# Preparing the state-space parameters of a two-block transformer: phase tables grouped ahead of the matrices, their stores on GpSimd's queue, and another buffer for the transposed weights

## The chip, the core and the metric

One core of a Trainium2 chip runs the whole program in one launch. The time is device microseconds of that core, the median of several executions. One further execution is recorded by the hardware profiler; all rows shown are from that one. Engines: PE is TensorE's matmul, PEld its weight load, DVE is VectorE, ACT is ScalarE, POOL is GpSimd, SP is SyncE, which here only issues DMAs.

## The reference

Two blocks of two layers each work on a sequence of 512 tokens, 2048 wide. The first block has an attention layer (gated linear attention beside "forgetting" attention) and then a diagonal state-space layer, S5; the second block has a recurrent layer and a latent-attention layer. The change concerns only the parameters of S5: 128 groups of 16 channels, each with a complex diagonal state of 64.

```python
def s5_ssm(u, lam_re, lam_im, log_step, b_re, b_im, c_re, c_im, d):
    lr = jnp.minimum(lam_re, -1e-4); li = lam_im
    step = jnp.exp(log_step)[:, None]
    mag = jnp.exp(lr * step)
    lb_re, lb_im = mag * jnp.cos(li * step), mag * jnp.sin(li * step)
    den = lr * lr + li * li
    nr, ni = lb_re - 1.0, lb_im
    coef_re = (nr * lr + ni * li) / den
    coef_im = (ni * lr - nr * li) / den
    bb_re = coef_re[..., None] * b_re - coef_im[..., None] * b_im
    bb_im = coef_re[..., None] * b_im + coef_im[..., None] * b_re
    ...  # x_t = lb * x_{t-1} + bb u_t (complex), y_t = Re(c x_t) + d u_t
```

All of lb, coef, bb and the powers of lb depend on weights alone, so the kernel can prepare them while an earlier layer still runs.

## The kernel before

**Staging.** Almost all time goes to projections, 2048-wide matrix products in split fp32r: a weight piece `wraw` (256 KB) is loaded by SP (line 265), ACT writes its rounded part and DVE the remainder into `whl` (`wpiece`, `split`: ACT first, then DVE), and PE makes three products from hi and lo parts into PSUM tiles `pj`. `wraw` has 3 buffers, `whl` 4, `pj` 4. `chunkF` uses two `pj` tiles at a time; `chunkT` uses all four. When a chunk is done, DVE or ACT evacuates it (`ha<-pj,bc` for queries and keys, `ge<-pj,bc` for gates).

**Order.** The program is traced in the order of the Python calls; a planner then fixes the order on each engine and DMA queue ahead of time, with its own durations: it takes, whenever an engine is free in its plan, the earliest traced instruction that is ready. Each engine and each queue works strictly in that order. A DMA issue is an instruction of its engine: it waits, at its place, for the data that it stores or for the buffer that it fills, and all behind it waits too. Tiles of one tag share that tag's buffers; the next user waits until the last reader of the old tile is done, DMAs included.

**The work around the change.** In the attention layer `layer_ab` calls a hook `beside(o)`, which is `params(o)` in `emit`, at fixed places: o = 0 before the first output gates; o = 1 to 8 in a loop over four pairs of forgetting-attention heads (`fox(i)`, then o = 1+2i; then two gate chunks for i = 1, 2 and `fox_in(i+1)`, the projections of the next pair, for i < 3; then o = 2+2i); o = 9 to 12 after each of the last four gate chunks; and o = 13 to 20 after each of the eight chunks of the output projection `w_out`. `params` makes three kinds of work:

- `s5_params` (o = 0), on GpSimd mostly: angles, powers, coefficients; a transposed weights table (`W` through PE into `wrow`, tag `ha` with 8 buffers, stored by 16 small DMAs from ACT's queue at line 930); and 16 rows of a table `s5tab` in DRAM, staged in `wt` and stored by GpSimd (line 983).
- `s5_tables(b0)`, eight calls: loads two rows of `s5tab` into the one buffer `lm` (SP, line 995), and for each of two batches DVE makes a table of cosines `C` and one of sines `Sn` (four products of 512 columns from `lm` into `cst` and `acc`, one subtraction and one addition into `hc`, 4 buffers). ACT's queue stores both (lines 1011 and 1012) as `s5ph`.
- `s5_batch_params(b)`, sixteen batches, in two halves. First half: loads (SP, lines 1023 to 1032), matrices on GpSimd through `cst` and `hc`, stored by GpSimd itself (line 1051), on DVE through `acc2`, and `BB` in the tag `fac` (one buffer). Second half: 32 small matmuls on PE that read `fac` (listed as tr<-vs,fac and tr<-acc,fac), and stores. It is traced at the next call, bound behind the last `chunkF` matmul that was traced before (`net.last`). A batch holds two of the four `vs` buffers.

`lm` also holds the masks of the gated linear attention; their last use is before the forgetting attention begins.

Of the kernel before, what the change touches and what calls it, by code (L numbers as in the profile page):

```python
# [22 lines left out]
P = 128  # L23
# [76 lines left out]
class Net:  # L100
# [723 lines left out]
    def s5_params(self):  # L824


        nc, I, A = self.nc, self.I, ALU
# [90 lines left out]
        for half in range(2):  # L918
            pw_ = self.ps("tr")
            for i in range(2):  # L920
                for j in range(2):
                    s_ = 2 * half + j
                    o = (2 * i + j) * P
                    self.tr(pw_[0:64, o:o + P], N[8 + i] if s_ == 3 else W[:, i, s_])
            wrow = self.t("ha", [64, 2, 2, P])
            self.act(wrow.rearrange("p i j f -> p (i j f)"), pw_[0:64])
            for j in range(2):
                for gg in range(2):
                    for i in range(2):
                        nc.scalar.dma_start(self.wtab[:, gg, 2 * half + j, i],  # L930
                                           wrow[:, i, j, 64 * gg:64 * gg + 64])
# [58 lines left out]
    def s5_tables(self, b0):  # L990


        nc, A = self.nc, ALU
        tab = self.t("lm", [P, S])[:, 0:384].rearrange("p (b f) -> p b f", b=2)
        self.dma.dma_start(tab, self.s5tab[b0:b0 + 2, :, 0:192].rearrange("b p f -> p b f"))
        for b in range(2):
            Tb = tab[:, b, 0:128].rearrange("p (i n q) -> p i n q", i=2, q=4)
            Ta = tab[:, b, 128:192].rearrange("p (i n q) -> p i n q", i=2, q=4)
            C, Sn = self.hd("hc"), self.hd("hc")
            u = [self.t("cst", [P, S]), self.t("acc", [P, S])]  # L1000
            v4 = lambda ap: ap.rearrange("p (q a b) -> p q a b", q=4, a=8)
            av = lambda i: Ta[:, i].rearrange("p n q -> p q n").unsqueeze(3).to_broadcast([P, 4, 8, 16])
            bv = lambda i: Tb[:, i].rearrange("p n q -> p q n").unsqueeze(2).to_broadcast([P, 4, 8, 16])
            self.tt(v4(u[0]), av(0), bv(0), A.mult)
            self.tt(v4(u[1]), av(1), bv(1), A.mult)
            self.tt(C, u[0], u[1], A.subtract)
            self.tt(v4(u[0]), av(0), bv(1), A.mult)
            self.tt(v4(u[1]), av(1), bv(0), A.mult)
            self.tt(Sn, u[0], u[1], A.add)
            d = self.dp.tile([P, 2, S], F32, name=self.name("s5ph"))  # L1010
            nc.scalar.dma_start(d[:, 0], C)
            nc.scalar.dma_start(d[:, 1], Sn)
            self.s5ph.append(d)

    def s5_batch_params(self, b):
# [533 lines left out]
def emit(nc, tc, I, col, out, layers=("ab", "c", "even", "odd")):  # L1549
    with ExitStack() as ctx:  # L1550
        net = Net(nc, tc, ctx, I, col)
        raws = net.load_x(I["x"])
        tok = bc = fac = acc2 = None
        second = "even" in layers or "odd" in layers
        last = layers[-1]
        end = lambda name: dict(store=False) if name == last else {}


        pending = []

        def params(o):


            if o == 0:
                net.s5_params()
            elif o <= 8:
                net.s5_tables(2 * (o - 1))
            for b in pending:
                with net.after([net.last]):
                    next(b, None)  # L1570
            pending.clear()
            if 3 <= o < 19:
                pending.append(net.s5_batch_params(o - 3))
                next(pending[0])
        if "ab" in layers:
            h = net.layer_ab(raws, beside=params if "c" in layers else None)
            raws, acc, _ = net.w_out(h, I["ab_w_out"][0], beside=params if "c" in layers else None, **end("ab"))
        else:
            acc = net.sumsq(raws)
        if "c" in layers:  # L1580
            if "ab" not in layers:
                net.s5_params()
                for b in range(16):
                    if b % 2 == 0:
                        net.s5_tables(b)
                    for _ in net.s5_batch_params(b):
                        pass
            h = net.layer_c(raws, acc)
            raws, acc, acc2 = net.w_out(h, I["c_w_out"][0], perm=True, fold="fin_g" if second else None, **end("c"))
        if second:  # L1590
            if acc2 is not None:
                t1 = net.rsqrt(net.colsum(acc), D)
                fac = net.bcast(t1, net.t("fac", [P, S]))
                sq = net.t("tk", [P, 4])
                net.tt(sq, t1, t1, ALU.mult)
                tok = net.rsqrt(net.colsum(acc2), D, mul=sq)
                net.tt(tok, tok, t1, ALU.mult)
                bc = net.bcast(tok)
            else:
                tok, bc = net.norm(acc)  # L1600
            if "even" in layers:
                h = net.layer_even(raws, tok, bc)
                raws, acc, _ = net.w_out(h, I["l0_w_out_2"], fac=fac, **end("even"))
                fac = None
                tok, bc = net.norm(acc) if "odd" in layers else (None, None)
            if "odd" in layers:
                h = net.layer_odd(raws, tok, bc)
                raws, acc, _ = net.w_out(h, I["l1_w_out_2"], fac=fac, **end("odd"))
        net.final_out(raws, acc, "fin2" if second else "fin_g", out)
# [12 lines left out]
```

## Time and profile before

| | |
|---|---|
| median of 3 runs | 3428.4 us (3428.11 to 3428.41) |
| profiled execution: its time | 3427.85 us |
| profiled execution: span of its instructions | 3426.1 us |
| mean granted TensorE clock | 0.995 |
| busy share PE, PEld, DVE, ACT, POOL | 98%, 82%, 56%, 39%, 23% |
| instructions | 49372 |

A busy PE is not always a PE at its peak, since the ends of matmuls are modelled; so what a stage loses is read from the stretches in which PE is not busy, from the named waits of PE, and from the granted clock. The S5 parameters are prepared between about 328 and 965 us of the span.

### The profile page before, as it was taken

The page shows a single profiled execution, that of the slowest core. Times are in us where ns is not written, and L with a number is a line of the kernel's source. Part 1 is how long each engine was busy: PE and PEld are TensorE (multiplying, and loading weights), DVE is VectorE, ACT ScalarE, POOL GpSimd, SP SyncE. Part 2 cuts the span into 40 slices and gives each one's busy share as a digit, 9 for nine tenths or more (in the row PEclk, how much of TensorE's full clock was granted, in tenths as well). Part 3 has the DMA queues.
Part 4 walks back from the last instruction along what each step waited for, and adds up shares of the span by engine and source line. Part 5 has one row for each costly group of instructions (what it writes and reads, how often), then busy time and mean ns, then how long its engine had stood idle before and what let it go on. Part 6 is the DMA issues. An engine that isn't in the chain of part 4 may idle for free.

```text
span 3426.1 us, 49372 instructions
## 1 busy us (share of the span) xinstructions
PE 3359.1 (98%) x18156; PEld 2812.7 (82%) x18156; DVE 1905.6 (56%) x3213; ACT 1336.7 (39%) x2497; POOL 786.3 (23%) x974
## 2 busy tenths in 40 slices
PE   8999989999999999999999999999999999999997
PEld 7898678877899989888888777888888888888885
DVE  5763674588567665734345655453545545646534
ACT  4443232233343333423343554232434444445422
POOL 0341851158614222100122010012110121112011
PEclk9999999999999999999999999999999999999998
DMA  5223354576734444333443223334333223232333
GB/s 149 75 63 88 99 157 121 146 211 194 220 118 145 133 135 127 114 120 118 135 135 96 69 70 86 96 119 143 108 87 83 66 75 80 79 82 78 110 118 108
DMA packets 407203, 390.23 MB, mean 114 GB/s; under 512 B 66713, under 2 KB 364057, under 8 KB 406961
## 3 DMA queue, kind: packets, MB, share of 16 engines
q1 hardware_dynamic: 381168, 354.64, 36.2%
q10 hardware_dynamic: 22464, 22.12, 1.9%
q0 software_dynamic: 3328, 10.32, 0.8%
q8 instruction: 142, 2.33, 0.3%
q14 instruction: 101, 0.82, 0.1%
HBM read 340.71 MB, written 46.25 MB: 113 GB/s over the span
## 4 chain that ended last, share of the span: by engine, by line
PE 83%; DVE 6%; POOL 4%; DMA 3%; issue 2%; ACT 1%; SPq 0%; DVEq 0%; ACTq 0%; POOLq 0%
PE pj L152 74%; PE sc L152 4%; PE po L152 3%; PE tr L156 1%; DVE whl L140 1%; DVE wk L140 1%; POOL vs L140 1%; DVE acc L140 1%; POOL hc L140 1%; DMA gated<-ge 1%; DMA wraw<-in_ab_w_in_dram 1%; POOL fac L140 1%; POOL cst L140 0%; PE tr L152 0%; POOL acc L140 0%
## 5 line engine op out<-in xcount | busy, mean ns | idle before, releaser
L152 PE MATMUL pj<-hl,whl 128*128 128x512 f32 x10224 | 2453.2, 398 | 12.3 <-ACT whl L137 6.9
L152 PEld LDWEIGHTS pj<-hl,whl 128*128 128x128 f32 x10224 | 1911.8, 189 | 453.7 <-DVE whl L140 7.7
L140 DVE TENSOR_TENSOR whl<-wraw,whl 128x512 fp32r<-128x512 f32 (+2 forms) x1064 | 806.9, 762 | 1096.3 <-ACT whl L137 1090.4
L137 ACT ACTIVATE whl<-wraw 128x512 fp32r<-128x512 f32 (+2 forms) x1064 | 660.0, 623 | 1332.9 <-PE pj L152 1072.3
L152 PE MATMUL pj<-whl,hl 128*128 128x256 f32 (+1 forms) x3840 | 482.1, 286 | 11.3 <-DVE ha L140 7.0
L152 PEld LDWEIGHTS pj<-whl,hl 128*128 128x128 f32 x3840 | 470.2, 190 | 17.8 <-DVE ha L140 7.2
L140 POOL TENSOR_TENSOR acc<-acc,wt 128x512 f32<-128x512 f32 x73 | 103.2, 1421 | 851.5 <-ACT wt L137 850.3
L140 POOL TENSOR_TENSOR ha<-wk,ha 64x512 fp32r<-64x512 f32 x32 | 44.6, 1394 | 294.6 <-ACT ha L137 256.2
L140 POOL TENSOR_TENSOR wt<-wt,acc 64x508 f32<-64x508 f32 x32 | 60.4, 1888 | 186.1 <-DVE wt L140 115.7
L137 ACT ACTIVATE wk<-sc,sm 128x256 f32<-128x256 f32 (+3 forms) x160 | 79.5, 501 | 60.1 <-DVE sm L148 55.1
L140 POOL TENSOR_TENSOR wt<-ha,wk 128x256 f32<-128x256 f32 x72 | 63.2, 905 | 113.4 <-PE pj L152 60.2
L152 PE MATMUL po<-pt,vs 128*128 128x128 f32 x560 | 80.2, 276 | 0.6 <-ACT pt L137 0.6
L156 PE MATMUL tr<-ident,wk 128*128 128x128 f32 x416 | 72.3, 276 | 7.7 <-ACT pt L137 6.5
L152 PEld LDWEIGHTS po<-pt,vs 128*128 128x128 f32 x560 | 72.9, 192 | 3.4 <-ACT pt L137 1.0
L152 PE MATMUL sc<-ha,ha 128*128 128x128 f32 (+1 forms) x224 | 72.0, 392 | 2.5 <-DVE sm L525 2.3
L137 ACT ACTIVATE pt<-tr 128x384 f32<-128x384 f32 (+3 forms) x96 | 46.6, 485 | 70.6 <-PE tr L156 54.2
L521 DVE TENSOR_REDUCE sm<-sc 128x1 f32<-128x128 f32 (+3 forms) x96 | 45.9, 488 | 47.5 <-PE sc L152 46.7
L156 PEld LDWEIGHTS tr<-ident,wk 128*128 128x128 f32 x416 | 51.7, 141 | 24.9 <-ACT pt L137 8.9
L140 POOL TENSOR_TENSOR fac<-vs,smb 128x128 f32<-128x128 f32 x64 | 37.9, 610 | 146.5 <-PE tr L152 139.4
L137 ACT ACTIVATE ge<-ge 128x512 f32<-128x512 f32 x64 | 40.1, 627 | 71.6 <-DVE ge L140 54.1
L143 DVE SCALAR_TENSOR_TENSOR ge<-ge,ge 128x512 f32<-128x512 f32 x60 | 45.9, 765 | 38.5 <-ACT ge L137 38.1
L140 POOL TENSOR_TENSOR fac<-wt,acc 128x512 fp32r<-128x512 f32 x8 | 10.3, 1292 | 236.0 <-ACT acc L137 179.2
(316 smaller groups left out, 3036.0 us busy)
## 6 DMA issues: line engine op xcount, KB each, us to landing
wraw<-in_l_w_in_dram SPq DMA_DIRECT2D x272, 256.0 KB, 2.8
wraw<-in_ab_w_in_dram SPq DMA_DIRECT2D x216, 256.0 KB, 2.9
wraw<-in_c_w_in_dram SPq DMA_DIRECT2D x128, 256.0 KB, 3.0
wraw<-in_l_w_out_dram SPq DMA_DIRECT2D x128, 256.0 KB, 2.7
wraw<-in_ab_w_out_dram SPq DMA_DIRECT2D x64, 256.0 KB, 3.8
wraw<-in_glu_w_dram SPq DMA_DIRECT2D x64, 256.0 KB, 2.7
wraw<-in_c_w_out_dram SPq DMA_DIRECT2D x64, 256.0 KB, 2.7
wraw<-in_l_w_in_dram SPq DMA_DIRECT2D x128, 128.0 KB, 2.3
```

Source lines behind the costliest of these rows:

```text
L137: return self.nc.scalar.activation(out, in_, func, **kw)
L140: return (eng or self.nc.vector).tensor_tensor(out, a, b, op=op)
L143: return self.nc.vector.scalar_tensor_tensor(out, a, s, b, op0=op0, op1=op1, **kw)
L152: return self.nc.tensor.matmul(out, l, r, start=start, stop=stop)
L156: return self.nc.tensor.transpose(out, in_, self.ident[:k, :k])
L521: self.nc.vector.tensor_reduce(mx, pb[:, 0:w], axis=AX.X, op=ALU.max)
```

## The change

Three edits. The transposed weights table `wrow` takes the tag `lm` (one buffer) in place of `ha` (eight). The stores of C and Sn are issued by GpSimd in place of ACT. And the hook's calendar changes: two calls of `s5_tables` at each of o = 1 to 4 in place of one at each of o = 1 to 8; then the batches, one at each of o = 5 to 18 and two at o = 10 and 12, in place of one at each of o = 3 to 18. The second halves still follow at the next call (the last at o = 19).

```diff
--- before.py
+++ after.py
@@ -922,7 +922,7 @@
                     s_ = 2 * half + j
                     o = (2 * i + j) * P
                     self.tr(pw_[0:64, o:o + P], N[8 + i] if s_ == 3 else W[:, i, s_])
-            wrow = self.t("ha", [64, 2, 2, P])
+            wrow = self.t("lm", [64, 2, 2, P])
             self.act(wrow.rearrange("p i j f -> p (i j f)"), pw_[0:64])
             for j in range(2):
                 for gg in range(2):
@@ -1008,8 +1008,8 @@
             self.tt(v4(u[1]), av(1), bv(0), A.mult)
             self.tt(Sn, u[0], u[1], A.add)
             d = self.dp.tile([P, 2, S], F32, name=self.name("s5ph"))
-            nc.scalar.dma_start(d[:, 0], C)
-            nc.scalar.dma_start(d[:, 1], Sn)
+            nc.gpsimd.dma_start(d[:, 0], C)
+            nc.gpsimd.dma_start(d[:, 1], Sn)
             self.s5ph.append(d)
 
     def s5_batch_params(self, b):
@@ -1557,21 +1557,25 @@
 
 
         pending = []
+        todo = iter(range(16))
 
         def params(o):
 
 
             if o == 0:
                 net.s5_params()
-            elif o <= 8:
-                net.s5_tables(2 * (o - 1))
-            for b in pending:
-                with net.after([net.last]):
-                    next(b, None)
-            pending.clear()
-            if 3 <= o < 19:
-                pending.append(net.s5_batch_params(o - 3))
-                next(pending[0])
+            elif o <= 4:
+                for i in range(2):
+                    net.s5_tables(4 * (o - 1) + 2 * i)
+            else:
+                for p in pending:
+                    with net.after([net.last]):
+                        next(p, None)
+                pending.clear()
+                for _, b in zip(range(2 if o in (10, 12) else 1), todo):
+                    p = net.s5_batch_params(b)
+                    next(p)
+                    pending.append(p)
         if "ab" in layers:
             h = net.layer_ab(raws, beside=params if "c" in layers else None)
             raws, acc, _ = net.w_out(h, I["ab_w_out"][0], beside=params if "c" in layers else None, **end("ab"))
```

## Rows read from the trace of the kernel before

**Rows 1.** Busy time of each engine by stretch, whole core

```profile
core 0: us, PE busy (x) PEld busy (x) DVE busy (x) ACT busy (x) POOL busy (x), PEclk, DMA share, GB/s
414.00:470.00 56.00, 43.50 (x261) 38.06 (x260) 46.54 (x58) 10.96 (x20) 42.47 (x82) 0.94 0.55 161
470.00:575.00 105.00, 105.00 (x593) 89.85 (x592) 51.90 (x102) 32.71 (x67) 12.56 (x22) 1.00 0.42 119
575.00:740.00 165.00, 162.07 (x980) 134.45 (x979) 114.15 (x216) 53.52 (x119) 47.10 (x76) 1.00 0.60 172
740.00:850.00 110.00, 102.06 (x625) 78.48 (x625) 87.32 (x117) 34.23 (x71) 89.79 (x133) 0.98 0.66 200
850.00:980.00 130.00, 130.00 (x708) 104.41 (x707) 77.67 (x110) 51.28 (x85) 68.77 (x92) 1.00 0.61 193
```

**Rows 2.** Who waited for whom, 400 to 470 us (total, times, longest)

```profile
ACT whl L137 <- DVE hc L140: 25.3, 7, 6.7
...
DVE cst L140 <- DMA lm<-s5tab: 10.9, 3, 7.0
...
PE pj L152 <- DVE ha L140: 7.0, 1, 7.0
...
PE tr L156 <- ACT pt L137: 3.5, 2, 1.8
...
PE pj L152 <- DVE whl L140: 1.3, 1, 1.3
...
PE po L152 <- ACT pt L137: 0.6, 1, 0.6
```

**Rows 3.** Timeline, 442.8 to 453.5 us (start, duration)

```profile
442.87 0.37 SPq L995 DMA_DIRECT2D lm<-s5tab  x1
...
446.75 1.13 DVE L140 TENSOR_TENSOR cst<-lm 128x512 f32<-128x512 f32 x1 [2.59 <-DMA lm<-s5tab]
...
452.22 0.68 DVE L140 TENSOR_TENSOR ha<-pj,bc 128x512 f32<-128x512 f32 x1
...
452.96 0.79 PE L152 MATMUL pj<-whl,hl 128*128 128x256 f32 x2 [7.05 <-DVE ha L140]
```

**Rows 4.** Granted clock in two short stretches

```profile
451.00:458.00 7.00, 5.04 (x24) 5.04 (x25) 6.93 (x10) 0.29 (x2) 5.33 (x9) 0.51 0.54 180
802.50:806.00 3.50, 3.50 (x10) 2.70 (x10) 3.50 (x6) 0.00 (x0) 3.38 (x6) 0.51 0.47 157
```

**Rows 5.** Who waited for whom, 580 to 740 us

```profile
POOL hc L1043 <- DMA s5ph<-hc: 32.3, 7, 7.0
...
PE tr L156 <- ACT pt L137: 2.9, 3, 1.4
```

**Rows 6.** Who waited for whom, 740 to 850 us

```profile
PE tr L152 <- POOL fac L140: 6.1, 5, 2.3
```

**Rows 7.** Instructions on tile fac by stretch (32 matmuls of PE for each batch)

```profile
737.00:824.00 87.00, 4.68 (x224) 3.15 (x224) 0.00 (x0) 0.00 (x0) 22.19 (x36) 0.98 0.65 192
824.00:966.00 142.00, 3.03 (x192) 2.22 (x192) 0.00 (x0) 0.00 (x0) 22.34 (x36) 1.00 0.67 210
```

**Rows 8.** Instructions on tile hc (ns minimum, median, maximum)

```profile
L140 DVE TENSOR_TENSOR hc<-cst,acc x32: 674/688/724, 417.3 to 731.1; 128x512 f32<-128x512 f32 x32
```

**Rows 9.** Tile s5d: the GpSimd stores

```profile
L1051 POOL DMA_DIRECT2D s5d<-hc x32: 580/580/675, 483.1 to 934.6; - x32
```

**Rows 10.** Instructions on tile lm by stretch

```profile
414.00:470.00 56.00, 0.00 (x0) 0.00 (x0) 26.52 (x25) 0.00 (x0) 0.94 0.55 161
...
575.00:740.00 165.00, 0.00 (x0) 0.00 (x0) 32.66 (x31) 0.00 (x0) 1.00 0.60 172
```

**Rows 11.** DMA issues, 330 to 980 us: KB each, median us to landing

```profile
s5ph<-hc ACTq DMA_DIRECT2D x32, 256.0 KB, 3.0
s5d<-hc POOLq DMA_DIRECT2D x32, 256.0 KB, 3.3
```

**Rows 12.** Tile s5w: the small stores of wrow, from issue to landing

```profile
DMA to landing us min/median/max: 1.7/1.8/2.1
```

## Prediction

> **What bounds the kernel now.** I read the granted clock and the busy shares first: PE is busy 98% of the span, so a change off PE can give back only what PE waits for. Then busy time by stretch [rows 1] shows where. From 414 to 470 us PE works 43.50 of 56 us, from 575 to 740 us 162.07 of 165, from 740 to 850 us 102.06 of 110; at 470 to 575 and 850 to 980 us it works throughout. So the S5 preparation costs PE 12.5 + 2.9 + 7.9 = 23.3 us of waiting, in the first, third and fourth stretch. To that comes the clock: after the long waits it stood at 0.51, the lower of its two levels (1.2 of 2.4 GHz), in 451 to 458 and 802.5 to 806 us [rows 4], where PE worked 5.04 and 3.50 us; at full clock these would have taken about half, so 2.5 and 1.7 us more are lost. Some 27 us, 0.8%, is all that the change could touch.
>
> Then the named waits. In 400 to 470 us [rows 2] PE waits 3.5 + 0.6 us for ACT's `pt`, 7.0 us for DVE's evacuation `ha` and 1.3 us for DVE's `whl`. ACT itself waits 25.3 us, seven times, for DVE's `hc`: these are the stores of C and Sn, which stand in ACT's queue ahead of the weight pieces and the `pt` copies and hold them until DVE has computed the table. DVE waits 10.9 us for the load of `lm`. The timeline [rows 3] shows both meeting: SP can issue the `lm` load at 442.87, when the old table has been read; DVE stands 2.59 us for it, then does two more table products before it reaches the evacuation at 452.22, and PE has stood 7.05 us. In 580 to 740 us [rows 5] ACT costs PE another 2.9 us, and GpSimd stands 32.3 us for `hc` buffers that table stores still read. In 740 to 850 us [rows 6] PE waits 6.1 us, five times, for GpSimd's `fac`: from 737 to 824 us seven batches pass (224 matmuls at 32), one per 12.4 us, against six in 142 us afterwards, one per 23.7 us [rows 7].
>
> **The change part by part.**
>
> *Stores on GpSimd.* 32 issues leave ACT. What PE loses by ACT's standing, 3.5 + 0.6 + 2.9 = 7.0 us [rows 2, 5], goes. Bounds: nothing, if the `pt` copies turn out to be late by DVE's own work anyway, and 7.0 + 1.3 us, if the late `whl` was also due to ACT. I take -7.0, since all of these waits stand in stretches with tables and [rows 2] names one cause for ACT. GpSimd gets 32 issues at 0.58 us by its own store of the same shape [rows 9], 18.6 us, and now waits for DVE in ACT's stead. What hides that: between 470 and 575 us it is busy 12.56 of 105 us [rows 1], and PE waits for it only where a batch's second half comes. Cover gone, it is a rival below. Behind a waiting store on GpSimd stand the staging copies for `s5tab`, and for these SP's `lm` loads.
>
> The store lands 3.3 us after a GpSimd issue and 3.0 us after an ACT issue [rows 11]; with four `hc` buffers and some 3 us of DVE work for each, that difference is worth nothing here. The Trainium skill (DMA: Bandwidth & Descriptors, SWDGE vs HWDGE vs iDMA) speaks against this edit: GpSimd writes its descriptors by software into SBUF, can be locked out there by DVE, and starts about 0.4 us later than a store by ACT. By the rows the sum has nothing for it; by the page an estimate is 32 times 0.4, or 13 us, if no store were hidden, and the sum below would end at 3431.
>
> *All tables first.* The order in which calls are traced is not the order of execution: the planner had already put 25 of the 64 table products into 414 to 470 us, and left 31 for after 575 [rows 10]. So half of the tables stay where they were. What moves into 470 to 575 us is 32.66 us of products and 16 of the 32 sums and differences at 0.688 us [rows 8], together 43.7 us of DVE, which has 51.90 of 105 us there [rows 1]: it fits, at 91%. The price of such density is read from 414 to 470 us, where DVE is 83% busy. Nearest is the late `whl`, 1.3 us in 56, so 2.4 us in 105; lower bound nothing, as PE waits for nothing in that stretch now; upper bound another stall like that of [rows 3] with its half clock, 7.0 + 2.5 = 9.5 us, since at the end of `fox_in(2)` a key chunk again hands over to a value chunk that wants all four `pj` tiles. I take +2.4.
>
> The stall at 445 us itself: its cause is DVE's order and the single `lm` buffer, and both stay. I take 0; the bound is -9.5 us, as the planner now orders DVE afresh and one evacuation placed two products earlier is enough.
>
> *Batches later.* Two effects. Tables no longer share `hc` and `cst` with batches after 575 us: GpSimd's 32.3 us of standing goes. And the calendar changes. Before, the fourth and fifth batch came only after the last tables, at 737 us or later, and with the next five made seven in 87 us. Now batches 0 to 2 have their second halves traced behind the key chunk of `fox_in(3)`, the others behind the gate chunks 9 (batch 3), 10 (4), 11 (5 and 6) and 12 (7), and the first two chunks of `w_out` (8 and 9, then 10). So the same 87 us should hold five batches or six. GpSimd's need is at most 12.5 us for each: 68.77 busy us of 130 [rows 1], by 23.7 us. Seven in 87 us are just that, five leave 17.4 us for each. The seven cost 6.1 + 1.7 = 7.8 us of waits and half clock, 1.1 us for each. I leave that price on two batches, 6 and 9, the second of each pair: `BB` has one buffer, so their products start only when the batch before has passed PE. That is 2.2 us, a gain of 5.6. Bounds: -7.8 (none waits, as with one per 23.7 us) and +7.8 (twice the waits, if the pairs and the late start bunch them).
>
> *`wrow` in `lm`.* The second half's copy must wait until the first half's eight stores have landed, 1.8 us after their issue [rows 12], at the head of ACT's queue. `whl` pieces stand ahead, so 0; bounds 0 and +1.8. The first table load into `lm` comes long after. That two `ha` buffers come free is worth nothing: no wait for a free `ha` buffer is among PE's.
>
> **Sum**, from the profiled execution's own time, 3427.85 us (its span is 3426.1; 1.75 us lie around it): -7.0 + 2.4 + 0 - 5.6 + 0 = -10.2, so 3417.65; the median of the runs is 0.55 us above the profiled one, so 3418.2, and I say 3418, 0.3% faster. About 0.2%, 6.9 us, is what a measurement of this kernel can tell from no change.
>
> **Rivals.**
>
> *The stall at 445 us goes too.* For it: [rows 3], any later place of two products lifts it. Against: the `lm` load is as late as before. 3418.2 - 9.5 = 3408.7 us.
>
> *DVE becomes the bound: the stall comes a second time.* For it: the tables now fill DVE to 91% in 470 to 575 us, and the planner evidently puts products ahead of evacuations. Against: with two gate chunks and softmax in between, evacuations are traced earlier than tables 4 to 7 and so go first. A second stall in place of the 2.4 us: 3418.2 - 2.4 + 9.5 = 3425.3; with half of the batches' gain lost as well 3428. No change.
>
> *GpSimd's queue becomes the wait (slower).* A store that waits for DVE holds the staging copies behind it; an `s5tab` row comes late, SP's `lm` load waits, DVE stands at its head, and the evacuation behind it is late. ACT stood 25.3 us for DVE [rows 2]; GpSimd would stand as long, and if the staging is late by as much before 470 us, DVE stands up to 25.3 us more. PE took 7.0 of DVE's 10.9 us, 64%: +16.2. ACT's 7.0 us still goes: 3428.4 - 7.0 + 16.2 = 3437.6, at half of that delay 3429.5. It decides once the staging loses its lead over the table loads. Against: GpSimd is busy 42.47 of 56 us from 414 to 470 us [rows 1], so it can stand 13.5 us there and stage no later than now.
>
> *The edits do nothing*, because the planner orders all by readiness: half of the tables were early anyhow. But ACT's queue loses its 32 stores in any order, so I count this within "no change".
>
> **How the numbers follow.** Chances: the forecast 0.42, the stall at 445 us gone as well 0.20, a second stall or nothing 0.23, GpSimd's queue 0.15. The first two are faster by over 0.2% (below 3421.5): 0.62; same 0.23; slower 0.15. The forecast's own range is 3411 to 3422: the batches' bound of -7.8 with 2.4 us saved, and half of the batches' gain lost. The range for 8 in 10 reaches down to 3403 (3408.7, with the batches at their bound, 2.2, no price for density, 2.4, and the late `whl`, 1.3 us) and up to 3432 (the second stall at its worst, and the milder half of GpSimd's queue).
>
> **What would show it.** Right: no wait of ACT for `hc` and PE's waits for `pt` gone; all table products before about 590 us; one batch each 12 to 25 us from 658 us on, with PE's wait for `fac` at some 2 us; no half clock near 800 us. Wrong: PE waiting for `ha` or `whl` between 470 and 590 us with a half clock behind it; DVE's wait for `lm` well above 10.9 us, or GpSimd's staging stretching past 480 us; `fac` waits above 6.1 us after 770 us, where the pairs are.

## The result

| | before | after |
|---|---|---|
| median | 3428.3 us (4 runs, 3425.9 to 3428.4) | 3447.8 us (4 runs, 3447.1 to 3449.5) |
| profiled execution: span | 3426.1 us | 3445.3 us |
| mean granted TensorE clock | 0.995 | 0.991 |
| PE's waits for `fac` | 6.1 us, 5 times | 16.0 us, 7 times |

The ratio is 1.0062, 95% interval 1.0049 to 1.0074: slower by 0.6%, some 20 us, where 0.3% faster was forecast, and outside the range of 3403 to 3432 us.

### The profile page after: what moved, and what is told of

It is laid out like the page before. It is cut to its first block, busy times and chain, and to the rows that moved or that the text cites. A ratio compares the mean times of both kernels' runs of the same rounds, so it can differ in the third digit from the quotient of the medians.

```text
span 3445.3 us, 49408 instructions
## 1 busy us (share of the span) xinstructions
PE 3369.2 (98%) x18156; PEld 2819.2 (82%) x18156; DVE 1907.5 (55%) x3213; ACT 1339.3 (39%) x2497; POOL 802.6 (23%) x1006
## 4 chain that ended last, share of the span: by engine, by line
PE 71%; DVE 2%; DMA 1%; POOL 1%; issue 1%; ACT 0%; DVEq 0%; SPq 0%; ACTq 0%; POOLq 0%
PE pj L152 63%; PE sc L152 3%; PE po L152 3%; PE tr L156 1%; DMA gated<-ge 1%; DVE wk L140 1%; DVE whl L140 0%; DVE wk L1130 0%; PE tr L152 0%; POOL hc L140 0%; POOL fac L140 0%; DMA s5d<-hc 0%; POOL cst L140 0%; DVE sc L140 0%; DVE ha L143 0%
## 5 line engine op out<-in xcount | busy, mean ns | idle before, releaser
L148 DVE TENSOR_SCALAR wk<-wk,sm 128x256 f32<-128x256 f32 (+3 forms) x160 | 60.6, 392 | 4.7
```

The source lines that it names most:

```text
L148: return e.tensor_scalar(out, a, s1, None, op0=op0)
```

## The profile after

Busy time by stretch of the changed kernel, in the columns of [rows 1]:

```profile
414.00:470.00 56.00, 46.59 (x280) 41.20 (x279) 50.82 (x64) 9.86 (x18) 43.91 (x79) 0.88 0.54 163
470.00:575.00 105.00, 98.02 (x500) 80.47 (x499) 79.56 (x135) 29.91 (x62) 19.98 (x38) 0.97 0.50 143
575.00:740.00 165.00, 165.00 (x939) 139.39 (x939) 74.28 (x162) 56.32 (x117) 33.85 (x53) 1.00 0.47 130
740.00:850.00 110.00, 96.95 (x617) 74.54 (x616) 88.84 (x118) 34.15 (x70) 86.23 (x132) 0.92 0.66 198
850.00:980.00 130.00, 127.02 (x714) 100.98 (x713) 70.47 (x105) 37.07 (x71) 89.50 (x131) 0.99 0.66 209
```

PE no longer waits at 575 to 740 us (162.07 busy before). But at 470 to 575 us, where it had worked throughout, it now stands 7 us and its clock falls; at 740 to 850 us it stands 13 us in place of 8, at a mean clock of 0.92 in place of 0.98; and at 850 to 980 us another 3 us. So there are two places to explain, the tables' and the batches'.

Who waited for whom, 400 to 470 us, changed kernel (us in total, times, longest), beside [rows 2]:

```profile
DVE cst L140 <- DMA lm<-s5tab: 10.1, 3, 7.1
...
POOL s5ph L1011 <- DVE hc L140: 5.8, 3, 2.5
PE pj L152 <- DVE whl L140: 5.1, 3, 2.1
...
PE pj L152 <- DVE ha L140: 4.2, 1, 4.2
ACT whl L137 <- DVE hc L140: 2.9, 2, 2.1
```

ACT's standing for `hc` has gone from 25.3 to 2.9 us and PE's 4.1 us for `pt` are gone. The stall for `ha` is still there, shorter, but PE's wait for DVE's `whl` grew from 1.3 to 5.1 us. So PE's waits for ACT went and waits for DVE came in their place, in all 9.3 us instead of 12.4.

The same view, 470 to 580 us, where PE waited for nothing before:

```profile
POOL s5ph L1012 <- DVE hc L140: 19.9, 6, 5.1
...
PE tr L156 <- ACT pt L137: 4.0, 1, 4.0
...
DVE cst L140 <- DMA lm<-s5tab: 3.1, 3, 1.3
PE sc L152 <- DVE sm L525: 2.9, 2, 2.7
```

The timeline of the changed kernel ahead of the longer of these waits (start, duration):

```profile
509.04 0.27 PE L156 MATMUL tr<-ident,wk 128*128 128x128 f32 x1
...
509.07 5.60 PE L152 MATMUL pj<-hl,whl 128*128 128x512 f32 x23
...
514.65 1.05 DVE L140 TENSOR_TENSOR cst<-lm 128x512 f32<-128x512 f32 x1
...
515.62 1.06 DVE L140 TENSOR_TENSOR acc<-lm 128x512 f32<-128x512 f32 x1
...
516.67 0.68 DVE L140 TENSOR_TENSOR ge<-pj,bc 128x512 f32<-128x512 f32 x1
...
517.38 0.63 ACT L137 ACTIVATE ge<-ge 128x512 f32<-128x512 f32 x1 [2.54 <-DVE ge L140]
...
518.39 0.27 ACT L137 ACTIVATE pt<-tr 128x128 f32<-128x128 f32 x1
...
518.72 0.44 PE L156 MATMUL tr<-ident,wk 128*128 128x128 f32 x2 [4.04 <-ACT pt L137]
```

PE had transposed a tile of the softmax at 509.04 us. Its next transposes need the same PSUM tile, `tr`, of which there is one, and ACT copied it out only at 518.39. The copy stood in ACT's queue behind an activation of the gates, `ge<-ge`, which waited 2.54 us for DVE's evacuation of a gate chunk; and that evacuation stood in DVE's order behind two table products. The shorter wait is more direct: DVE's softmax step on the scores stands behind two products, the first of which waited 1.31 us for the load of `lm`.

```profile
478.25 1.06 DVE L140 TENSOR_TENSOR cst<-lm 128x512 f32<-128x512 f32 x1 [1.31 <-DMA lm<-s5tab]
...
479.22 1.05 DVE L140 TENSOR_TENSOR acc<-lm 128x512 f32<-128x512 f32 x1
480.20 0.28 DVE L525 CUSTOM_DVE_ANT_0 wk<-sc,hb 128x128 f32<-128x128 f32 x1
...
480.54 0.91 PE L152 MATMUL sc<-ha,ha 128*128 128x384 f32 x2 [2.67 <-DVE sm L525]
```

This is the forgetting attention of pair 1, a chain PE, DVE, ACT, DVE, PE, ACT, PE with little between its links. Its steps share the queues of DVE and ACT with evacuations, and the table products now run through it: on the tile `lm` the 32 products of `cst` start between 413.7 and 538.4 us in one run, where the kernel before left 31 of its 64 products for after 575 us [rows 10].

Instructions on tile `fac`, changed kernel, as in [rows 7] (32 matmuls of PE, column two, for each batch):

```profile
575.00:658.00 83.00, 0.00 (x0) 0.00 (x0) 0.00 (x0) 0.00 (x0) 3.53 (x6) 1.00 0.38 102
658.00:737.00 79.00, 0.51 (x32) 0.37 (x32) 0.00 (x0) 0.00 (x0) 3.11 (x6) 1.00 0.56 159
737.00:824.00 87.00, 4.90 (x224) 3.31 (x224) 0.00 (x0) 0.00 (x0) 20.35 (x36) 0.94 0.63 186
824.00:866.00 42.00, 1.70 (x72) 1.13 (x72) 0.00 (x0) 0.00 (x0) 8.11 (x17) 0.92 0.66 209
866.00:966.00 100.00, 2.52 (x152) 1.79 (x152) 0.00 (x0) 0.00 (x0) 18.00 (x33) 0.98 0.71 228
```

One batch passes before 737 us, where three were forecast; then seven in the same 87 us as before, and two more (and the start of a third) in the next 42 us, where the kernel before had one. PE's named wait between 740 and 990 us:

```profile
PE tr L152 <- POOL fac L140: 16.0, 7, 4.3
```

Three of the stretches in which the granted clock stood at its lower level (columns as above):

```profile
519.20:522.60 3.40, 3.40 (x11) 2.66 (x9) 3.40 (x5) 0.00 (x0) 0.17 (x1) 0.51 0.55 159
...
806.00:812.80 6.80, 5.94 (x39) 4.30 (x42) 6.80 (x6) 1.40 (x3) 6.61 (x13) 0.50 0.45 157
836.70:843.50 6.80, 5.91 (x21) 4.68 (x22) 4.21 (x4) 2.14 (x5) 5.72 (x11) 0.50 0.91 297
```

Each goes with a wait of PE of 4.0 to 4.3 us, ended at 518.7, 806.9 and 837.6 us. Between 414 and 990 us there are seven such stretches, 41 us in all, where the kernel before had two, 10 us.

**The loss by stretch.** To put waits and clock into one number I took, for each matmul in the trace, the time from its start to the next one's start, less the median of that for the same operation and shape in the kernel before, and summed the excess. It is worked out from the one profiled execution of each kernel:

| us | 414 to 470 | 470 to 575 | 575 to 740 | 740 to 990 | 990 to 1420 | all other |
|---|---|---|---|---|---|---|
| before | 16.0 | 2.4 | 10.1 | 17.9 | 8.9 | 55.2 |
| after | 13.9 | 13.5 | 5.3 | 34.1 | 6.9 | 54.8 |
| difference | -2.1 | +11.1 | -4.9 | +16.2 | -2.0 | -0.3 |

The sum is +18.0 us, of the 19.2 us by which the span grew.

## The experiments

Each was timed beside the kernel before on the same chip; "above before" is the difference of the two medians, the ratio has its 95% interval, the losses are worked out as above, and `fac` is PE's named wait between 740 and 990 us.

| kernel | above before, us | ratio | loss 470 to 575 | loss 740 to 990 | `fac` |
|---|---|---|---|---|---|
| the change | +19.5 | 1.0062 (1.0049 to 1.0074) | 13.5 | 34.1 | 16.0 |
| x1 stores alone | +3.7 | 1.0009 (1.0000 to 1.0019) | 3.7 | 23.6 | 7.6 |
| x2 calendar alone | +21.6 | 1.0057 (1.0042 to 1.0072) | 12.8 | 32.9 | 17.0 |
| x3 `wrow` alone | +0.3 | 1.0001 (0.9992 to 1.0010) | | | |
| x4 tables dense, batches as before | +12.7 | 1.0037 (1.0024 to 1.0050) | 18.3 | 19.9 | 5.6 |
| x5 tables as before, batches late | +19.2 | 1.0055 (1.0040 to 1.0070) | 7.6 | 30.8 | 14.0 |
| x6 change, half the matrices | +6.4 | 1.0018 (1.0009 to 1.0028) | 13.2 | 16.7 | 5.2 |
| x9 change, half the products | +6.8 | 1.0020 (1.0010 to 1.0029) | 2.9 | 29.3 | 14.1 |
| x10 change, call 7 ahead | +15.7 | 1.0044 (1.0028 to 1.0061) | 16.4 | 23.1 | 8.1 |
| x12 change, pairs late | +20.6 | 1.0063 (1.0051 to 1.0076) | 16.0 | 25.0 | 11.6 |
| x14 x10 and x12 together | +16.2 | 1.0051 (1.0038 to 1.0065) | 14.0 | 19.6 | 6.9 |
| x7 before, batches earlier | -2.4 | 0.9994 (0.9985 to 1.0003) | 5.2 | 18.6 | 5.7 |
| x8 x7 and GpSimd stores | +0.2 | 1.0000 (0.9991 to 1.0009) | 4.4 | 21.6 | 6.4 |
| x11 x7 and call 7 ahead | +3.1 | 1.0007 (0.9999 to 1.0016) | 6.2 | 18.2 | 5.7 |
| x13 x7 with a free place | -3.6 | 0.9988 (0.9979 to 0.9997) | 5.4 | 14.6 | 2.6 |

### The three edits, one by one

x1 is the second part of the diff alone, x3 the first, x2 the third.

> The kernel before with one edit: GpSimd issues the 32 stores of C and Sn. Theory (the stores are harmless; late batches and dense tables cost the time): ACT's waits for hc and PE's 7.0 us of waits for pt go, 3420 to 3428 us. Rival (a store that waits on GpSimd's queue holds the staging and the batches behind it): 3435 us or more, with PE's waits for fac well above 6.1 us.

> The kernel before with one edit: the calendar (two table calls at o = 1 to 4, batches from o = 5). Theory: the whole loss is here, 3444 to 3455 us: PE waits some 16 us for fac after 740 us, and ACT's stores add to PE's waits for pt in the denser tables. Rival (the loss is that of the stores on GpSimd): 3428 us within 7.

> The kernel before with one edit: wrow in the tag lm. Theory: worth nothing, 3425 to 3431 us. Rival (ACT stands at its queue's head for the first half's stores and delays weight pieces): up to 1.8 us more, and the planner's new order may move more than that, either way.

x2 and x3 came as expected: the calendar alone costs the whole 20 us, and `wrow` nothing. x1 missed: its +3.7 us can hardly be told from no change, but nothing was gained. Its waits of PE, 400 to 470 us:

```profile
PE pj L152 <- DVE whl L140: 5.1, 3, 2.1
PE pj L152 <- DVE ha L140: 4.2, 1, 4.2
```

The 4.1 us for `pt` are gone and 3.8 us more for `whl` have come, in the same order as in the changed kernel; the low clock there lasts 13.7 us (438.7 to 452.4) in place of 6.8. With the batches as before, the stretch of 740 to 990 us also loses 5.7 us more. Its waits for `fac` are 7.6 us in place of 6.1, 5.8 of them in a single one at 800 us, and the low clock lasts 10.2 us in place of 3.4. x4 and x8, which share the GpSimd stores, have a single wait of 5.6 and 5.3 us. Why the order planned for the batches then has one long wait in place of several short ones wasn't separated.

### Tables or batches

x4 keeps the dense tables and calls the batches at o = 3 to 18 again:

```diff
-            else:
-                for p in pending:
...
+            for b in pending:
+                with net.after([net.last]):
+                    next(b, None)
+            pending.clear()
+            if 3 <= o < 19:
+                pending.append(net.s5_batch_params(o - 3))
+                next(pending[0])
```

> The changed kernel with the batches traced where they were before (one at each of o = 3 to 18), tables still two a call at o = 1 to 4, stores on GpSimd, wrow in lm. Theory (the late batches are the larger cost: after 737 us 15 of them are left in place of 13, because the second halves behind fox(3) cannot pass it): PE's wait for fac falls from 16.0 to about 6 us and the half clocks after 770 us to one, 3428 to 3436 us. Rival (the dense tables, 11 us in 470 to 575, are the larger cost): 3440 us or more.

x5 is its mirror image, on the kernel before (stores and `wrow` too):

```diff
-            if 3 <= o < 19:
-                pending.append(net.s5_batch_params(o - 3))
-                next(pending[0])
+            if o > 4:
...
+                for _, b in zip(range(2 if o in (10, 12) else 1), todo):
...
```

> The kernel before with the second half of the calendar alone: batches from o = 5 with pairs at 10 and 12; tables one call at each of o = 1 to 8, stores on ACT, wrow in ha. Theory (after fox(3) GpSimd is the bound, and two batches more are left for it): 7 to 13 us over the kernel before, PE waits for fac 14 us or more, the stretch 470 to 575 us as quiet as before. Rival (late batches cost only because the dense tables delay the first of them): within 5 us of before.

Each half alone costs more than 12 us, and the two do not add up: 12.7 and 19.2 us alone, 21.6 together (x2). x4 has the waits of its theory, `fac` at 5.6 us and the batches' loss near that of before (19.9), but 12.7 us above before is the time of its rival, whose 3440 us lay 12 us above the 3428 us that the kernel before had measured when this was written. The tables' loss is even higher, as the first batches now fall into the dense tables (DVE 86.04 of 105 us busy at 470 to 575 us, GpSimd 34.20 in place of 19.98). x5 cost more than I had expected, and its rival is out. It lost 7.6 us at 470 to 575 us too, where I had expected quiet: with no batches to compete, 41 of the 64 table products lie before 495 us (30 in the kernel before), and PE waits 2.5 us for an evacuation by ACT that stands behind the stores in ACT's queue.

### Which engine sets the pace

x6 leaves out one of the two input matrices of each batch (five GpSimd instructions; the first is stored twice). x9 leaves out the second pair of products of each table, so that Sn is the sum of the first pair. Both start from the changed kernel.

```diff
+            if i == 0:
                 o = self.hd("hc")
...
+            for gg in range(2 if i == 0 else 0):
```

> The changed kernel; of each batch's two input matrices only the first is computed, and stored twice (five GpSimd instructions of each batch, some 4 of its 12 us, are left out; the stores stay). Theory (GpSimd's work per batch is the bound after 740 us): PE's wait for fac falls from 16 us to under 5 and the time by 10 to 16 us, to 3431 to 3438 us by the clock of before. Rival (the waits are latency of loads and hand-overs between PE, ACT and DVE, not GpSimd's work): under 5 us gained.

```diff
-            self.tt(v4(u[0]), av(0), bv(1), A.mult)
-            self.tt(v4(u[1]), av(1), bv(0), A.mult)
```

> The changed kernel; the second pair of products of each table is left out (the sine table is the sum of the first pair), so DVE's table work falls from 90 to 56 us while calendar, loads and stores stay. Theory (DVE's density in 414 to 575 us makes the softmax and the weight pieces late): PE's loss in 470 to 575 us falls from 13.5 to under 5 us, and the time by 8 to 14 us; PE's wait for fac stays near 16 us. Rival (the 11 us there come from the stores or the single lm buffer): under 4 us gained.

The two causes separate, and both gains are clear of noise. Less GpSimd work brings the time from 19.5 to 6.4 us above before, nearly all of it behind 740 us (34.1 to 16.7), and leaves the tables' loss at 13.2; the waits stay just above the 5 us expected. PE's wait in x6, 740 to 990 us:

```profile
PE tr L152 <- POOL fac L140: 5.2, 4, 1.7
```

Less DVE work brings it to 6.8 us above before: the loss at 470 to 575 us is gone (2.9), while `fac` stays at 14.1 us. The single `lm` buffer is not what was cured, since DVE still waits 2.2 us for its loads from 470 to 580 us (3.1 in the changed kernel). Busy time of x9 in that stretch, with DVE at 60.34 in place of 79.56 us:

```profile
470.00:575.00 105.00, 104.95 (x578) 88.93 (x577) 60.34 (x122) 32.82 (x71) 13.19 (x26) 1.00 0.51 144
```

### Why only one batch passed before 737 us

GpSimd and PE in the changed kernel, around the pass of batch 1 (timeline):

```profile
696.46 0.46 POOL L140 TENSOR_TENSOR fac<-fac 128x128 f32<-128x128 f32 x1
...
741.58 0.14 POOL L1080 MEMSET vs<- 128x48 f32 x1 [26.87 <-PE po L152]
742.07 0.94 POOL L140 TENSOR_TENSOR fac<-vs,smb 128x128 f32<-128x128 f32 x2 [0.35 <-PE tr L152]
```

```profile
740.46 1.06 PE L152 MATMUL po<-pt,vs 128*128 128x128 f32 x8
741.44 0.32 PE L152 MATMUL tr<-vs,fac 128*32 128x16 f32 x16
```

The last `fac` product of batch 1 is done at 696.9 us, and PE reads it at 741.4, at the end of `fox(3)`: 44 us later. GpSimd stands for 26.9 us of these behind the batch's second half. The second half writes a PSUM tile of tag `tr`, of which there is one (`tr=1`, line 111), and so do the transposes of `fox(3)`. The second half of batch 1 is traced at o = 7, behind `fox(3)`, so its turn on `tr` comes after them. PE's own order does not hold it: between the transposes of `fox(3)` PE makes the gate chunks that are traced behind call 7, as here, while batch 1 waits:

```profile
712.79 0.60 PE L156 MATMUL tr<-ident,wk 128*128 128x128 f32 x4
...
713.81 4.65 PE L152 MATMUL pj<-hl,whl 128*128 128x512 f32 x19
...
719.19 0.27 PE L156 MATMUL tr<-ident,wk 128*128 128x128 f32 x1
719.22 5.36 PE L152 MATMUL pj<-hl,whl 128*128 128x512 f32 x22
```

x10 traces that one call ahead; the `chunkF` matmul that it is bound behind (`net.last`) stays the same:

```diff
+            if i == 3:
+                beside(1 + 2 * i)
             fox(i)
-            beside(1 + 2 * i)
+            if i < 3:
+                beside(1 + 2 * i)
```

> The changed kernel with call o = 7 traced before fox(3) in place of after it. Theory (the second half of batch 1 was ready at 697 us and waited until 741 because its tr bank is given out in traced order, behind fox(3)'s transposes): batch 1 passes PE before 715 us, batch 2 is first behind fox(3), PE's wait for fac falls to 9 to 13 us, the time by 3 to 8 us. Rival (what holds batch 1 is its own data or the vs buffers): it still passes at about 740 us and nothing changes.

The timeline of PE in x10:

```profile
698.76 0.26 PE L152 MATMUL tr<-vs,fac 128*32 128x16 f32 x8
...
703.43 0.26 PE L152 MATMUL tr<-vs,fac 128*32 128x16 f32 x8
...
709.35 0.27 PE L156 MATMUL tr<-ident,wk 128*128 128x128 f32 x1
```

Batch 1 passes at 699 to 703 us, `fac` falls to 8.1 us, even below what was expected, and the loss behind 740 us from 34.1 to 23.1. The time comes only from 19.5 to 15.7 us above before, and the two intervals overlap: in this profiled execution the tables' loss is 2.9 us higher and that at 990 to 1420 us 2.0 us, which takes part of the gain. So x10 shows what holds the batch, and how long; what that costs in time is read from its profile alone. A run with a second `tr` tile was not made.

### How the batches should lie

x7 asks whether it is the number of batches behind `fox(3)` that costs, with all of them one call earlier in the kernel before; x8 adds the GpSimd stores, x11 the edit of x10.

```diff
-            if 3 <= o < 19:
-                pending.append(net.s5_batch_params(o - 3))
+            if 2 <= o < 18:
+                pending.append(net.s5_batch_params(o - 2))
```

> The kernel before, with every batch called one hook earlier (o = 2 to 17 in place of 3 to 18); all else as before. Theory (what costs is the number of batches left behind fox(3), each wanting some 12 us of GpSimd): the second half of batch 3 is now traced before fox(3) and passes PE before 700 us, twelve batches are left after 737 us in place of thirteen, PE waits for fac less than 3 us in place of 6.1, and the half clock near 802 us goes; 5 to 8 us below the kernel before, a ratio near 0.998. Rival (the first batch lies among the tables and the forgetting attention, and costs PE there what it saves later): the same time or slower, with PE's waits before 640 us up by 5 us or more.

> The kernel before, with every batch called one hook earlier and the table stores on GpSimd. Theory: the stores are worth nothing on either side (alone they made no difference), so within 3 us of the run with the earlier batches alone. Rival (ACT's waits for pt, 7.0 us, come back as a gain once the batches leave room, as the prediction had it): 5 to 7 us below that run.

> The kernel before, with every batch called one hook earlier and the hook call o = 7 traced ahead of fox(3) in place of behind it. Theory: batch 4 passes PE before 725 us too, so eleven batches are left after 737 us and PE waits for fac less than 2 us; 1 to 4 us below the run with the earlier batches alone. Rival (GpSimd is the bound already before 737 us, as it shares hc with the table stores there): batch 4 is not ready in time, and the time is that of the earlier batches alone or up to 4 us above it, since PE then waits for fac in front of fox(3).

None of the three is measurably faster than before. In x7 one batch fewer is left behind 737 us, but the places at which PE takes them, from 737 to 821 us, are filled as before, by seven, and PE waits 5.7 us in place of 6.1. So the number left in all isn't it, and this theory falls. In x8 the stores are again worth nothing that can be measured. x11 met neither side: batch 4 does pass early, at 690 us, and only five are left for 737 to 824 us (160 matmuls), yet `fac` stays at 5.7 us and the time is 5.5 us above x7's, more than its rival allowed. Instructions on tile `fac` in x11:

```profile
737.00:824.00 87.00, 3.65 (x160) 2.38 (x160) 0.00 (x0) 0.00 (x0) 17.56 (x30) 0.92 0.64 193
```

The next theory was how close the second halves stand. x13 takes one place out of the crowd; x12 moves the pairs of the changed kernel to where PE comes by every 23 us; x14 joins x12 and x10.

```diff
-            if 3 <= o < 19:
-                pending.append(net.s5_batch_params(o - 3))
+            if 2 <= o < 19 and o != 8:
+                pending.append(net.s5_batch_params(o - 2 - (o > 8)))
```

> The kernel before, with the batches called at o = 2 to 7 and 9 to 18, so that one of the crowded places (the gate chunk at o = 9) brings no second half. Theory now (how close the second halves stand): six batches in place of seven between 737 and 824 us, 25 us between the two around the free place; PE waits for fac less than 3 us in place of 6.1 and one half clock near 780 or 800 us goes; 4 to 8 us below the kernel before, a ratio near 0.998. Rival (GpSimd stands still until fox(3) has passed and what it then has to catch up costs the same in any calendar): fac stays near 6 us, and the time is that of the earlier batches alone, 3422 to 3425 us.

```diff
-                for _, b in zip(range(2 if o in (10, 12) else 1), todo):
+                for _, b in zip(range(2 if o in (15, 17) else 1), todo):
```

> The changed kernel with its two pairs of batches at o = 15 and 17 in place of 10 and 12, so that the calls while the output gates end and w_out begins bring one batch each. Batch 1 still passes PE at 741 us, and as many batches are left behind fox(3) as in the changed kernel. Theory now (what costs is how close the second halves stand in PE's order between 737 and 866 us against GpSimd's 11 to 12 us for each, not how many are left in all): seven batches between 737 and 824 us in place of eight, then one per 23 us, as before the change; PE's waits for fac fall from 16.0 us to 6 to 8, the half clock behind 815 us goes, and the time is 7 to 12 us below the changed kernel (3436 to 3441). Rival (the number left behind fox(3) costs, as the run with the early batches was to show): fac stays at 12 us or more and the time within 4 us of the changed kernel.

> The changed kernel with the hook call o = 7 ahead of fox(3) and its two pairs of batches at o = 15 and 17: the two edits that have each been run alone. Theory (two causes that add up: fox(3) holds back batch 1, and the early pairs crowd the second halves): PE's waits for fac fall to 5 us or less (16.0 in the changed kernel, 8.1 and 11.6 with one edit each), the loss behind 740 us is that of the kernel before, and what stays above the kernel before is the dense tables' loss at 470 to 575 us: 8 to 13 us above it, a ratio of 1.0023 to 1.0038. Rival (both edits take away the same waits, or GpSimd's late start costs the same whatever the calendar): fac stays at 8 us or more, and the ratio is 1.004 or above.

x13 has the waits that the theory says: six batches between 737 and 824 us, one low clock of 3.4 us in place of x7's two, and this wait of PE, 740 to 990 us:

```profile
PE tr L152 <- POOL fac L140: 2.6, 2, 2.3
```

At 3.6 us, or 0.12% below the kernel before, it is the only one whose interval lies wholly below 1: a small gain, less than the 0.2% named in the prediction, a little short of the 4 to 8 us of its theory, and not told apart from x7, whose interval overlaps with its own. x12 has the time of its rival and a wait between the two sides: `fac` fell only to 11.6 us. Its crowd between 737 and 824 us has six batches, where the changed kernel has seven (one less on either side than I had counted). They wait 9.1 us, no less than the seven of the kernel before (6.1), and the late pairs another 2.5. Its profiled execution was 4.8 us shorter than the changed kernel's, its ratio is not lower. x14 brings the loss behind 740 us to 19.6, near the 17.9 of before, as the theory of two causes says; `fac` at 6.9 us lies between the theory's bound and the rival's, and the ratio, 1.0051, meets the rival. Its profiled execution took 3438.1 us, at the upper end of the theory's 8 to 13 above before, but its five runs go from 3436.7 to 3447.1 us, those of the changed kernel from 3447.1 to 3449.5. Where that scatter comes from stays open. In x12 and x14 some 4 us of what is won behind 740 us is lost again at 990 to 1420 us (10.6 and 11.1, where the changed kernel loses 6.9). So how much the pairs cost stays open, and so does the price of a crowd: five batches wait 5.7 us (x11), six wait 2.6 (x13) or 9.1 (x12), seven 5.7 or 6.1 (x7 and before).

## Why the prediction was wrong

**Stores on GpSimd, -7.0.** ACT's standing went as forecast, but alone this gave no gain (x1, +3.7 us, at the edge of what can be told from no change). The lower bound, nothing because DVE is late anyway, was the nearest at 414 to 470 us: waits for DVE's `whl` took the place of those for `pt`. At 575 to 740 us the loss did fall, by 4.9 us with the change and 3.5 with x1, but x1 gave it back behind 740. GpSimd as the wait, the rival, did not come: DVE's wait for `lm` is 10.1 us up to 470 us, against 10.9 before [rows 2], and 3.1 us behind it. The Trainium skill (DMA: Bandwidth & Descriptors, Latency and other measured facts) gives about 1 us to the first byte of a DMA issued by GpSimd and 0.6 us of one by ACT, so as an estimate a GpSimd store is 0.4 us later. The landings under the new calendar agree in the direction, 2.7 us from GpSimd (after) against 2.1 from ACT (x2), and those under the old do not, 2.8 (x1) against 3.0 [rows 11]; no run shows a loss of time by it.

**All tables first, +2.4.** The mechanism, density of DVE, was named; its size was 11.1 us, above the bound of 9.5, though DVE was busy 76% there and not 91%. The place was wrong. I looked for a late evacuation between two chunks of `fox_in(2)` and took the row nearest to that, `whl`. The stretch also holds the forgetting attention, and both long waits stand in it: one directly behind DVE's softmax step, one through ACT, whose copy out of `tr` stood behind a gate evacuation that DVE made too late. Ahead of either stood two table products of 1.1 us, and a half clock came with both. x9 shows that it is DVE's work: with half of the products the loss is 2.9.

**The stall at 445 us, 0.** It stayed, at 4.2 in place of 7.0 us, but with twice the half clock; 414 to 470 us as a whole lost 2.1 us less.

**Batches later, -5.6: the step that failed.** It measured +16.2 us at 740 to 990 us. The argument was that what kept the fourth and fifth batch until 737 us was the tables, by the `hc` and `cst` that they share, so that without tables batches 0 to 2 would pass before and "the same 87 us should hold five batches or six". They held seven, as before, and the crowd went on behind them. What held batches at 690 to 737 us was `fox(3)`, through the one `tr` tile that is given out in traced order: shown by x10, where one call traced ahead lets batch 1 pass some 40 us earlier. x4 shows that it was not the tables: none is left behind 550 us there, and the fourth batch, called as before, still waits from 703 to 748 us. GpSimd and PE in x4 (timeline):

```profile
702.52 0.46 POOL L140 TENSOR_TENSOR fac<-fac 128x128 f32<-128x128 f32 x1
...
747.89 0.32 PE L152 MATMUL tr<-vs,fac 128*32 128x16 f32 x16
```

The trace of the kernel before had shown it already: its fourth batch was done on GpSimd at 691 us and passed PE at 739.3. And in the view of [rows 5], 580 to 740 us, the longest wait of all is GpSimd's for PE to take the batch before, not the 32.3 us for `hc` that I read:

```profile
POOL fac L140 <- PE tr L152: 58.1, 3, 44.3
```

Taking the tables out of 575 to 740 us only made GpSimd idle there: 33.85 us busy in place of 47.10 [rows 1]. And since no batch had passed between 575 and 658 us, where two did before (64 matmuls), ten came between 741 and 866 us, where the kernel before has eight, seven of them close together; GpSimd's instructions on one take some 12 us together, and it waited up to 4.9 us for a load of `vs`. x4 (batches back: 19.9) and x6 (less work for each: 16.7) show the same from both sides. How the price follows from the number in the crowd is not shown.

**`wrow`, 0.** Right (x3).

**The rivals.** "DVE becomes the bound" came true as a mechanism, a second stall of 4.0 us and another of 2.7, but it had been priced beside gains that did not come. The lower end of the forecast's own range was added up wrongly, too: 2.2 and 2.4 us below 3418.2 is 3413.6 and not 3411.

## What to carry to other kernels

Small matmuls slipped in between others can only pass where their PSUM tile's turn comes: for each hook, ask which single-buffered tile the code traced ahead of it still wants, before asking which engine is free. And look at every long wait of the engine that makes them ready, the ones for PE too. Work that fills an engine to 76% was not hidden where the same engine is a link in a chain that PE waits for; at 57% it was (x9). A place beside projections alone might hide it better, but no run here tried that. And moving background work later takes away the head start that hides its slowest engine. Counting the pieces in the crowded places warns of that, but did not give the price here.

## What the runs showed of the hardware

PE's waits cost more than their length. With each wait of PE of 2.4 us or more between 470 and 990 us in the changed kernel (six, the longest 4.3) the granted clock stood at 0.50, 1.2 of 2.4 GHz, for 3.4 to 6.8 us; of the 16.2 us lost at 740 to 990 us, 9.9 us are named waits for `fac` (16.0 less 6.1), and most of the rest is matmuls at that level, which lasted 20.4 us there in place of 3.4. GpSimd issued a store of 256 KB in 0.54 us, in the midst of DVE's products, no slower than its own stores before [rows 9].
